# The first output tile stored in one piece, and the early small writes of the output removed, in a masked softmax

## Chip, cores, metric

The kernel runs on one core of one Trainium2 chip. The time is the device time of a run in microseconds (us). A trace is of one profiled run; its span is about 1.8 us shorter than the run's time.

## The reference

Sixteen batches of 8 x 256 rows of 256 numbers; batch b is softmaxed over its first `lengths[b]` columns (128 to 255), and the rest is zero.

```python
for b in range(batch):
    length = lengths[b]
    masked = x[b, :, :, :length].copy()
    masked = masked - np.max(masked, axis=-1, keepdims=True)
    exp_masked = np.exp(masked)
    result[b, :, :, :length] = exp_masked / np.sum(exp_masked, axis=-1, keepdims=True)
```

The input has 33.6 MB and the output too. The kernel reads 28.5 MB of the one, as most tiles are loaded only up to the column needed, and writes all of the other.

## The kernel before

A batch is one tile: 128 partitions, each with `nt` = 16 rows of 256 numbers, 16 KB per partition and 2 MB in all. There are 8 slots. SP loads tiles 0 to 3 and then issues all the stores, everything on one DMA queue (queue 1). GpSimd loads tiles 4 to 15 on another (queue 0). VectorE masks and divides, ScalarE takes the exponential.

How a tile's store is cut decides the packet size: a half of a tile is 8 KB in a row of each partition, a quarter 4 KB, a whole tile 16 KB.

```python
def parts(b):
    if b < 10:
        cuts = [0, half, half + quarter, nt]
    elif b < 12 or b == batch - 1:
        cuts = [0, half, nt]
    else:
        cuts = [0, nt]
    return [slice(i, j) for i, j in zip(cuts, cuts[1:])]
```

The small writes at the top: sixteen times 64 B into the region of tile 0, before anything else is written.

```python
out_e = out_f[0].rearrange("(e r) t k -> e r t k", e=few)[:, 0, 0, :few]
nc.vector.memset(touch, 0.0).then_inc(s_zero, 1)
nc.scalar.wait_ge(s_zero, 1)
nc.scalar.dma_start(out=out_e, in_=touch).then_inc(s_touch, 16)
# [SP's loads of tiles 0 to 3 left out]
nc.sync.wait_ge(s_touch, 16)
for b in range(batch):
    s_b = s_st[b % 2]
    for s in parts(b):
        nc.sync.wait_ge(s_out, 2 * b + (s.stop - 1) // half + 1)      # divided by VectorE
        if b >= 2 and s.start == 0:
            nc.sync.wait_ge(s_b, 64 * (b // 2 + 1))                    # the store of tile b - 2
        nc.sync.dma_start(out=out_f[b, :, s, :], in_=xt[:, b % slots, s, :]
                          ).then_inc(s_b, 16 * ((s.stop - s.start) // quarter))
```

VectorE's order: it masks tile b + 1 (and so waits for that tile's load) before it divides tile b.

```python
for b in range(batch):
    if b == 0:
        divide(0, 0)
    if b + 1 < batch:
        mask(b + 1, slice(0, nt))
    if b > 0:
        divide(b, 0)
    divide(b, 1)
```

The softmax here doesn't subtract the row's maximum and nothing guards it: scores larger than these inputs give would overflow.

## Time and profile before

| | before |
|---|---|
| time, median of 3 runs | 156.84 us (156.65 to 157.08) |
| span of the profiled run | 155.0 us |
| busiest compute engine | VectorE, 74% |
| DMA queues 1 and 0, share of the 16 engines' time | 66.2% and 32.0% |
| mean rate | 400 GB/s |

The two shares of the queues are the row to look at: added, they are 98% of all the time that the 16 DMA engines have. The lines themselves stand in the prediction.

### The profile page before, as it was taken

The page shows a single profiled execution, that of the slowest core. Times are in us where ns is not written, and L with a number is a line of the kernel's source. Part 1 is how long each engine was busy: PE and PEld are TensorE (multiplying, and loading weights), DVE is VectorE, ACT ScalarE, POOL GpSimd, SP SyncE. Part 2 cuts the span into 40 slices and gives each one's busy share as a digit, 9 for nine tenths or more (in the row PEclk, how much of TensorE's full clock was granted, in tenths as well). Part 3 has the DMA queues.
Part 4 walks back from the last instruction along what each step waited for, and adds up shares of the span by engine and source line. Part 5 has one row for each costly group of instructions (what it writes and reads, how often), then busy time and mean ns, then how long its engine had stood idle before and what let it go on. Part 6 is the DMA issues. An engine that isn't in the chain of part 4 may idle for free.

```text
span 155.0 us, 1322 instructions
## 1 busy us (share of the span) xinstructions
PE 0.2 (0%) x1; PEld 0.1 (0%) x1; DVE 115.1 (74%) x85; ACT 105.2 (68%) x514; POOL 19.0 (12%) x25
## 2 busy tenths in 40 slices
PE   0000000000000000000000000000000000000000
PEld 0000000000000000000000000000000000000000
DVE  1249999957999894949889499999894999950000
ACT  3087799993989694793959488989695798800000
POOL 4910031002020201102020112020100000000000
DMA  4999999999999999999999999999999999999993
GB/s 112 421 452 419 444 309 374 417 429 435 403 409 396 411 413 407 429 407 411 410 413 420 404 419 403 408 412 412 425 405 449 420 419 429 440 435 435 416 419 129
DMA packets 10452, 62.08 MB, mean 400 GB/s; under 512 B 930, under 2 KB 1026, under 8 KB 7122
## 3 DMA queue, kind: packets, MB, share of 16 engines
q1 hardware_dynamic: 6336, 41.95, 66.2%
q0 software_dynamic: 4080, 20.12, 32.0%
q14 instruction: 2, 0.02, 0.0%
q10 hardware_dynamic: 34, 0.00, 0.0%
HBM read 28.51 MB, written 33.56 MB: 400 GB/s over the span
## 4 chain that ended last, share of the span: by engine, by line
DMA 66%; DVE 15%; issue 5%; POOLq 2%; SPq 1%; DVEq 0%
DMA xt<-in_x_dram 58%; DVE xt L231 10%; DMA out_dram<-xt 8%; DVE xt L204 5%; DVE inv_sum L228 1%; SPq L117 1%; POOLq L144 0%; POOLq L139 0%; POOLq L101 0%; SPq L119 0%; SPq L127 0%; DVEq L221 0%; POOLq L166 0%; POOLq L162 0%; POOLq L168 0%
## 5 line engine op out<-in xcount | busy, mean ns | idle before, releaser
L258 ACT ACTIVATE xt<-xt x256 | 102.4, 401 | 27.7 <-DVE xt L204 27.7
L231 DVE TENSOR_TENSOR xt<-xt,inv_sum 128x2048 f32<-128x2048 f32 x32 | 73.3, 2292 | 1.1
L204 DVE SCALAR_TENSOR_TENSOR xt<-down,len_s,xt 128x2048 f32<-128x2048 f32 (+1 forms) x17 | 37.8, 2224 | 18.3 <-DMA xt<-in_x_dram 18.2
L258 ACT ACTIVATION_READ_ACCUMULATOR xt<-xt x256 | 47.9, 187 | 0.0
L139 POOL DMA_DIRECT2D xt<-in_x_dram x12 | 12.8, 1064 | 90.0 <-DMA out_dram<-xt 50.4
L228 DVE RECIPROCAL inv_sum<-row_sum 128x8 f32<-128x8 f32 x32 | 6.3, 196 | 1.1 <-ACT xt L258 1.1
L158 POOL MEMSET xt<- 128x1536 f32 x4 | 5.3, 1386 | 1.1 <-DVE len_s L195 1.1
L250 ACT ACT_TABLE_LOAD x1 | 1.3, 1283 | 2.1 <-DVE touch L112 2.1
L112 DVE MEMSET touch<- 16x16 f32 x1 | 0.1, 72 | 1.2 <-SPq L79 1.2
L187 DVE TENSOR_SCALAR down<-iota_i 128x256 f32<-128x256 int32 x1 | 0.3, 297 | 0.3 <-POOL iota_i L150 0.3
L192 DVE CAST len_b<-word 1x16 bf16<-1x16 int32 x1 | 0.2, 163 | 0.4 <-DMA word<-in_lengths_dram 0.4
L195 DVE TENSOR_SCALAR len_s<-len_f 128x16 f32<-128x16 f32 x1 | 0.2, 173 | 0.3 <-PE len_f L174 0.3
L150 POOL IOTA iota_i<- 128x256 int32 x1 | 0.3, 331 | 0.6 <-SPq L79 0.6
L155 POOL MEMSET seed<- 1x1 f32 x2 | 0.3, 162 | 0.0
L250 ACT ACTIVATE warm<-const-float32-0.0 128x1 f32<-128x1 f32 x1 | 0.2, 203 | 0.0
L153 POOL MEMSET ones<- 1x128 bf16 x1 | 0.2, 194 | 0.0
L174 PE MATMUL len_f<-len_b,ones 1*128 1x16 bf16 x1 | 0.2, 166 | 2.6 <-DVE len_b L192 2.6
L276 POOL MEMSET const-float32-0.0<- 128x1 f32 x1 | 0.1, 98 | 0.3 <-issue 0.3
L174 PEld LDWEIGHTS len_f<-len_b,ones 1*128 1x128 bf16 x1 | 0.1, 100 | 2.6 <-POOL ones L153 2.6
L276 POOL MEMSET const-bfloat16-1.0<- 128x1 bf16 x1 | 0.1, 99 | 0.0
L276 POOL MEMSET const-uint8-127<- 128x1 uint8 x1 | 0.1, 99 | 0.0
L276 POOL MEMSET const-float32-1.0<- 128x1 f32 x1 | 0.1, 98 | 0.0
(1 smaller groups left out, 0.0 us busy)
## 6 DMA issues: line engine op xcount, KB each, us to landing
out_dram<-xt SPq DMA_DIRECT2D x16, 1024.0 KB
out_dram<-xt SPq DMA_DIRECT2D x20, 512.0 KB
xt<-in_x_dram SPq DMA_DIRECT2D x3, 2048.0 KB, 16.1
out_dram<-xt SPq DMA_DIRECT2D x3, 2048.0 KB
xt<-in_x_dram POOLq DMA_DIRECT2D x3, 1728.0 KB, 16.2
xt<-in_x_dram POOLq DMA_DIRECT2D x2, 2048.0 KB, 16.2
xt<-in_x_dram POOLq DMA_DIRECT2D x2, 1600.0 KB, 14.2
xt<-in_x_dram POOLq DMA_DIRECT2D x2, 1280.0 KB, 13.6
```

Source lines behind the costliest of these rows:

```text
L117: nc.sync.dma_start(out=xt[:, 0, s], in_=x_f[0, :, s]).then_inc(s_ld[h], 16)
L139: nc.gpsimd.dma_start(out=xt[:, slot, :, :w], in_=x_n[:, n, :, :w]).then_inc(s_sw[par], 16)
L150: nc.gpsimd.iota(iota_i, pattern=[[1, seq_k]], base=0, channel_multiplier=0).then_inc(s_iota, 1)
L155: nc.gpsimd.memset(seed[:, par : par + 1], 0.0).then_inc(s_st[par], 64)
L158: nc.gpsimd.memset(xt[:, b, :, low:], 0.0).then_inc(s_fill, 1)
L174: nc.tensor.matmul(len_f, lhsT=ones, rhs=len_b, start=True, stop=True).then_inc(s_lenf, 1)
L204: return nc.vector.scalar_tensor_tensor(out=t, in0=down[:, None, lo:hi].to_broadcast([P, s.stop - s.start, hi - lo]), scalar=len_s[:, b : ...
L228: step(nc.vector.reciprocal(out=inv_sum[:, b, s], in_=row_sum[:, b, s]))
L231: nc.vector.tensor_tensor(out=t, in0=t, in1=inv_sum[:, b, s, None].to_broadcast([P, half, seq_k]), op=ALU.mult,).then_inc(s_out, 1)
L250: nc.scalar.activation(out=warm, in_=nc.const_aps.tensor(0.0, (P, 1), F32), func=EXP)
L258: ins = nc.scalar.activation(out=e, in_=e, func=EXP, accum_out=sum_h[:, bass.ds(i, 1), j])
L276: nc = _bacc.Bacc("TRN2", target_bir_lowering=False, num_devices=1)
```

## The change

Its intent: fewer and larger packets for the first tile's store, and no writes at the top that serve nothing but to be early. The diff, cut to its core:

```diff
     def parts(b):
-        if b < 10:
+        if b == 0:
+            cuts = [0, nt]
+        elif b < 10:
             cuts = [0, half, half + quarter, nt]
...
-    few = 16
-    touch = pool.tile([few, few], F32, name="touch")
...
-        out_e = out_f[0].rearrange("(e r) t k -> e r t k", e=few)[:, 0, 0, :few]
-        nc.vector.memset(touch, 0.0).then_inc(s_zero, 1)
-        nc.scalar.wait_ge(s_zero, 1)
-        nc.scalar.dma_start(out=out_e, in_=touch).then_inc(s_touch, 16)
...
-        nc.sync.wait_ge(s_touch, 16)
         for b in range(batch):
```

More of the change, by code (lines that the diff above doesn't have):

```diff
@@ L82 @@
         s_ones = sem("s_ones")
-        s_touch = sem("s_touch")
-        s_zero = sem("s_zero")
         s_lenb = sem("s_lenb")
```

## The prediction

> **What bounds the kernel now.** I read the page's two share lines first, then the windows by stage, then the waits of the store queue, and last the transfers around the first store.
>
> The busy shares, then the slices of the DMA engines:
>
> ```profile
> PE 0.2 (0%) x1; PEld 0.1 (0%) x1; DVE 115.1 (74%) x85; ACT 105.2 (68%) x514; POOL 19.0 (12%) x25
> ...
> DMA  4999999999999999999999999999999999999993
> GB/s 112 421 452 419 444 309 374 417 429 435 403 409 396 411 413 407 429 407 411 410 413 420 404 419 403 408 412 412 425 405 449 420 419 429 440 435 435 416 419 129
> ...
> q1 hardware_dynamic: 6336, 41.95, 66.2%
> q0 software_dynamic: 4080, 20.12, 32.0%
> ```
>
> No compute engine is over 74% busy, while the 16 DMA engines are at nine tenths or more in every slice but the first and the last. Queue 1 carries the first four loads and all stores, queue 0 the GpSimd loads; together they hold 98% of the engines' time. So the end is set by the sum of DMA work, unless a queue runs dry. The windows (stretch, length, busy time of five engines, clock, DMA share, GB/s) show one hole only:
>
> ```profile
> 2.00:20.00 18.00, 0.17 (x1) 0.10 (x1) 11.26 (x10) 11.43 (x51) 5.33 (x4) 1.00 1.01 412
> 20.00:24.00 4.00, 0.00 (x0) 0.00 (x0) 3.93 (x5) 4.00 (x21) 1.29 (x1) 1.00 0.92 281
> 24.00:152.00 128.00, 0.00 (x0) 0.00 (x0) 99.53 (x70) 89.77 (x444) 11.48 (x11) 1.00 1.02 417
> 125.50:152.00 26.50, 0.00 (x0) 0.00 (x0) 12.30 (x10) 8.78 (x44) 0.00 (x0) 1.00 1.01 429
> ```
>
> From 20 to 24 us the engines move 281 GB/s instead of about 415 (share 0.92: they are mostly occupied, but each packet takes longer). That loses (415 - 281) x 4 / 415 = 1.3 us. The first-tile store lies exactly behind it in queue 1. The last row is 26.5 us of stores alone: at the end a deep backlog drains.
>
> Waits of the store queue, over the whole span and then from 120 us on, and the last work of VectorE:
>
> ```profile
> SPq L126 <- DMA out_dram<-xt: 100.5, 14, 11.6
> SPq L127 <- DVE xt L231: 11.6, 6, 4.2
> SPq L124 <- DVE xt L231: 10.2, 1, 10.2
> ...
> SPq L126 <- DMA out_dram<-xt: 28.7, 5, 11.4
> SPq L131 <- DMA out_dram<-xt: 8.1, 1, 8.1
> ...
> 135.64 2.29 DVE L231 TENSOR_TENSOR xt<-xt,inv_sum 128x2048 f32<-128x2048 f32 x1
> 138.92 6.42 SPq L127 DMA_DIRECT2D out_dram<-xt  x3
> ```
>
> SP mostly waits for the store two tiles earlier (L126), hardly for compute. VectorE ends at 135.64 + 2.29 = 137.9 us, and by the last row the final stores are issued up to 138.92 + 6.42 = 145.3 us: the last tile had been ready some 6 us before it was let go. L124, the first wait of SP for compute, took 10.2 us and hurt nobody, as the loads were still running. No row waits at L121 for the small writes: that wait was over before SP came to it.
>
> **What the Trainium skill says.** "HBM Reference", Access, puts one core streaming alone at about 425 GB/s, bounded by its 16 DMA engines; the 429 above agrees. "DMA: Bandwidth & Descriptors", Why small descriptors are slow, gives every packet a small fixed overhead. The trace agrees, and it is tiny at these sizes (sizes below). The same page, Queues, rings and completion order, says that each engine goes round-robin over its queues, switching at packet boundaries; with both queues loaded the trace has packets one for one:
>
> ```profile
> q0 software_dynamic: 193, 0.93, 56.9%
> q1 hardware_dynamic: 195, 0.73, 44.9%
> ```
>
> (DMA queues, 27 to 31 us: queue, packets, MB, share.) So a queue's share of the bytes goes with its packet size. The page speaks of packets of several descriptors; the rows here are single contiguous runs (4096 B of a store, 4800 B of a load).
>
> **The change, part by part.**
>
> Packets: a row of the tile is 16 KB per partition, 8 partitions per DMA engine. The time of a packet, from windows with one size in them: 138 to 142 us has 104 packets of 16 KB at 99.4% of 16 x 4 us, so 0.612 us each; 127.8 to 130 us has 114 of 8 KB at 100.6% of 16 x 2.2 us, so 0.310; 41 to 41.4 us has 42 of 4 KB at 105.8% of 16 x 0.4 us, so 0.161. The first tile's store costs an engine now 8 x 0.310 + 16 x 0.161 = 5.06 us, afterwards 8 x 0.612 = 4.90. Saved: 0.16 us, on the bound.
>
> Small writes: 16 writes of 64 B and their 16 completions, on queue 10. The DMA queues between 5.3 and 6.7 us, and their issue:
>
> ```profile
> q10 hardware_dynamic: 32, 0.00, 1.4%
> ...
> out_dram<-touch ACTq DMA_DIRECT2D x1, 1.0 KB, 5.3
> ```
>
> 1.4% of 1.4 us is 0.02 us of each engine. The 5.3 us to landing were spent queueing behind the loads, beside which nothing waits. Saved: 0.02 us. The removed VectorE memset (72 ns), and ACT's issue before its table load, lie in a time when both only wait for the first tile. Saved: nothing.
>
> Issues: two SP issues fewer, 0.4 us each, off the path. The one store now waits for both halves (divided by 18.7 us) instead of starting at 14.1. But queue 1 holds four loads ahead of it until about 23.4 us (8 MB from 2.2 us, with the slow stretch), so it starts when it did.
>
> Moved: from about 26.3 us the first GpSimd load shares the engines. Now it meets 64 KB of 4 KB packets, 16 turns an engine until 31.8 us. Afterwards the store is down to about four packets of 16 KB then; the load gets 4 turns in 4 x (0.612 + 0.185) = 3.2 us, then tile 1's 8 KB packets. Its 21 packets an engine (1600 KB / 16 / 4800) then end about 2.5 us later than the 35.6 us of now, and the store of tile 0 about 2.3 us earlier. The bytes are the same, so this is a swap of order.
>
> Sum of what is certain: -0.16 - 0.02 = -0.18 us, or 156.66.
>
> **Rivals.**
>
> First, a cold output. The small writes look put there to make the first access to the output early. Without them the real stores may begin with slow packets. For it: the first reads of the input were slow. Between 2 and 4 us the four half-microseconds moved 246, 147, 262 and 328 GB/s, a mean of 246, which against 429 loses 0.85 us (ramp included). Against it: the small writes themselves show no stall around them (416 GB/s in 5.3 to 6.7 us), and only 16 spots were touched. If it holds, an estimate of its cost is the same 0.85 us, so 157.5; 40%.
>
> Second, a wait that takes the freed one's place. The first GpSimd load lands 2.5 us later, VectorE waits for it longer than its 2.6 us of now, and everything behind shifts: up to +2.3 us, 159. Against it: the DMA engines have stores of tiles 1 to 3 to move meanwhile, and the final tile has some 6 us to spare. 10%.
>
> Third, the slow stretch from 20 to 24 us hangs on the stores waiting behind the loads, and goes or shrinks with their new form: up to -1.3, so 155.5. For it: it ends where the stores begin. Against it: the first GpSimd issue falls in the same stretch (20.85 us) and stays. 12%.
>
> **Range and chances.** -0.18 + 0.4 x 0.85 + 0.1 x 2.3 - 0.12 x 1.3 = +0.23, which I round down: 157.0 us. The range is from the third rival, a little short of full, to the first with twice its estimated size: 155.9 to 158.5. Two per cent are 3.1 us: slower needs two rivals together, or a cold start of over 3 us, 4%; faster would need more than the whole hole at 20 us, 1%.
>
> **What would show it.** Right: queue 10 falls from 34 packets to 2, queue 1 loses 16 data packets, DMA stays at nine tenths in all middle slices, the last tile still waits for its predecessor's store. The swap: the first GpSimd load's time to landing grows from 14.7 to about 17 us, with the end unmoved. The cold output: GB/s between 23 and 28 us well under 400, packets of 16 KB over 0.612 us there. The prediction is wrong if the DMA share sinks anywhere behind 28 us, if the last store is issued straight from VectorE, or if the stretch from 20 to 24 us changes by over 1 us.

## The result

The changed kernel took 156.40 us (median of 4 runs, 156.32 to 156.85), the kernel before 156.80 beside it (4 runs). The ratio is 0.9978, with a 95% interval of 0.9954 to 1.0002. A ratio here is the mean time of one kernel's fast runs over the mean of the other's in the same rounds, so it is not quite the ratio of the medians. Executions over 1.5% slower than the fastest of the same kernel are left out of the means. By the 2% rule the two are the same; whether the small gain is real is a question for the experiments.

The page of the changed kernel, first engine shares, then the DMA slices, then the queues (queue, packets, MB, share):

```profile
PE 0.2 (0%) x1; PEld 0.1 (0%) x1; DVE 115.1 (74%) x84; ACT 105.2 (68%) x514; POOL 19.0 (12%) x25
...
DMA  4999999999999999999999999999999999999993
GB/s 108 430 445 424 436 309 416 409 411 436 423 404 388 423 405 416 412 412 422 398 421 412 411 413 404 414 409 412 417 409 450 417 420 426 443 432 436 424 415 144
...
q1 hardware_dynamic: 6048, 41.95, 66.1%
q0 software_dynamic: 4080, 20.12, 32.1%
...
q10 hardware_dynamic: 2, 0.00, 0.0%
```

Nothing has moved at this distance. VectorE has one instruction less (the memset). Queue 10 fell from 34 packets to 2, as the small writes were 16 data packets and 16 completions. Queue 1 has 6336 - 6048 = 288 packets less: 256 of data (16 engines times 24 before, times 8 now) and two completions per engine, 32. The prediction's list says "16 data packets", which is right per engine.

The same windows of the changed kernel (stretch, length, busy time of five engines, clock, DMA share, GB/s), and the waits of its store queue:

```profile
2.00:20.00 18.00, 0.16 (x1) 0.10 (x1) 11.25 (x10) 11.10 (x51) 5.33 (x4) 1.00 1.00 411
20.00:24.00 4.00, 0.00 (x0) 0.00 (x0) 3.93 (x5) 4.00 (x21) 1.71 (x2) 1.00 0.97 303
24.00:152.00 128.00, 0.00 (x0) 0.00 (x0) 99.62 (x70) 89.75 (x444) 11.09 (x11) 1.00 1.01 417
```

```profile
SPq L117 <- DMA out_dram<-xt: 98.9, 14, 9.6
SPq L118 <- DVE xt L222: 24.7, 7, 14.9
SPq L122 <- DMA out_dram<-xt: 8.2, 1, 8.2
```

The slow stretch at 20 to 24 us is still there, at 303 GB/s after 281, and all behind it runs at 417 as before. The first wait of SP for compute is now under L118, 14.9 us long in place of 10.2: the store waits for both halves of the tile, behind loads that still run, at no cost.

What did move is the first GpSimd load. The first row is VectorE's mask of tile 4 before the change, the second the same after it (in brackets: idle time of VectorE before it, and what ended it):

```profile
35.83 2.35 DVE L204 SCALAR_TENSOR_TENSOR xt<-down,len_s,xt 128x2048 f32<-128x2048 f32 x1 [2.62 <-DMA xt<-in_x_dram]
```

```profile
37.59 2.35 DVE L195 SCALAR_TENSOR_TENSOR xt<-down,len_s,xt 128x2048 f32<-128x2048 f32 x1 [4.40 <-DMA xt<-in_x_dram]
```

The load lands 1.8 us later, and VectorE waits 1.8 us longer. The reason shows in the queues from 26.2 to 29.2 us of the changed kernel:

```profile
q1 hardware_dynamic: 62, 0.92, 71.5%
q0 software_dynamic: 64, 0.31, 24.7%
```

The packets stand one for one, but queue 1's are 16 KB and queue 0's 4.8 KB, so the load gets a quarter of the engines' time instead of about half. And the end is where it was:

```profile
137.17 2.29 DVE L222 TENSOR_TENSOR xt<-xt,inv_sum 128x2048 f32<-128x2048 f32 x1
...
138.59 6.31 SPq L118 DMA_DIRECT2D out_dram<-xt  x3
```

VectorE ends at 139.5 us instead of 137.9, while the last stores still go out up to 144.9 us (145.3 before).

### The profile page after: what moved, and what is told of

It reads as the page before. It is cut to its first block, busy times and chain, and to the rows that moved or that the text cites. A ratio compares the mean times of both kernels' runs of the same rounds, so it can differ in the third digit from the quotient of the medians.

```text
span 154.7 us, 1317 instructions
## 1 busy us (share of the span) xinstructions
PE 0.2 (0%) x1; PEld 0.1 (0%) x1; DVE 115.1 (74%) x84; ACT 105.2 (68%) x514; POOL 19.0 (12%) x25
## 3 DMA queue, kind: packets, MB, share of 16 engines
q1 hardware_dynamic: 6048, 41.95, 66.1%
## 4 chain that ended last, share of the span: by engine, by line
DMA 71%; DVE 12%; issue 4%; POOLq 1%; SPq 1%; DVEq 0%
DMA xt<-in_x_dram 60%; DMA out_dram<-xt 11%; DVE xt L222 9%; DVE xt L195 3%; SPq L109 1%; POOLq L135 1%; DVE inv_sum L219 0%; POOLq L130 0%; SPq L111 0%; SPq L118 0%; POOLq L157 0%; POOLq L159 0%; DVEq L212 0%; POOLq L137 0%; SPq L278 0%
```

## The experiments

Twelve kernels ran in four batches, each batch on one chip beside runs of the kernel before. Times are medians; "before" is its median in the same batch.

| run | time (us) | before (us) | ratio to before, 95% interval | GB/s, 20 to 24 us |
|---|---|---|---|---|
| after_again | 156.53 | 156.84 | 0.9984 (0.9967 to 1.0001) | 324 |
| no_touch_only | 156.84 | 156.84 | 1.0006 (0.9987 to 1.0025) | 295 |
| whole_only | 156.88 | 156.84 | 1.0013 (0.9990 to 1.0036) | 336 |
| whole_first4 (5 fast runs) | 159.09 | 156.84 | 1.0157 (1.0119 to 1.0194) | 320 |
| gpsimd_later | 157.32 | 156.96 | 1.0029 (1.0006 to 1.0052) | 303 |
| stores_later | 158.06 | 156.96 | 1.0072 (1.0049 to 1.0095) | 292 |
| gpsimd_tiny_first | 156.85 | 156.96 | 0.9999 (0.9981 to 1.0018) | 315 |
| sp_touch | 156.92 | 156.79 | 0.9996 (0.9975 to 1.0017) | 332 |
| sp_touch_rows | 157.00 | 156.79 | 1.0004 (0.9981 to 1.0026) | 299 |
| tail_quarters | 157.30 | 156.79 | 1.0027 (1.0002 to 1.0051) | 332 |
| after_third | 156.55 | 156.97 | 0.9981 (0.9957 to 1.0006) | 315 |
| whole_first2 | 157.53 | 156.97 | 1.0029 (1.0003 to 1.0056) | 332 |

### The change again, and its two parts

after_again and after_third are the changed kernel as it is.

> The changed kernel once more, as the yardstick of this job. Theory (packets): the whole gain is the first tile's eight 16 KB packets in place of 8 KB and 4 KB ones, plus 0.02 us of small writes: 0.2 us under the kernel before, ratio 0.9987. The first reading (0.9978, or 0.35 us) would be partly chance. Rival (slow stretch): the change also shortens the stretch from 20 to 24 us (303 GB/s after 281), so 0.35 us again, with over 300 GB/s in it.

> The changed kernel a third time, since neither part alone showed its share and 0.2 us is near what five rounds can tell. Theory (packets): ratio 0.9988; with the first two readings (0.9978, 0.9984) the mean of the three stays below 1 but within 0.3 us of it. If it reads 1.000 or more, the first two were mostly chance of the run.

The three readings are 0.9978, 0.9984 and 0.9981, a mean of 0.9981, or 0.3 us of 156.8. Each interval taken alone just reaches past 1 (upper ends 1.0002, 1.0001 and 1.0006), but three batches agree. So the small gain is most likely real. It is so small, though, that kernels which differ from the changed one by a few small instructions (whole_only, gpsimd_tiny_first, sp_touch, sp_touch_rows, all below) read 0.9996 to 1.0013. Nor does it name its cause: after_again gained 0.25 us with 324 GB/s in the slow stretch, which lies between the two theories of its expectation (0.2 us, or 0.35 us with over 300 GB/s).

no_touch_only removes the small writes alone:

```diff
-        if b == 0:
-            cuts = [0, nt]
-        elif b < 10:
+        if b < 10:
```

(against the changed kernel).

> Only the small writes at the top are gone; the first tile is stored in three parts as before. Theory: 0.02 us of DMA work less, which no timing shows: ratio 1.000 within 0.001, and the windows from 23 to 28 us as in the kernel before. Rival (cold output): the first real stores are slow, packets of 8 KB above 0.31 us from 23 us on beyond the 0.33 to 0.42 us that the kernel before shows in its first microsecond, up to 0.85 us lost: ratio 1.005.

It took 156.84 us, as the kernel before did, and its windows from 24 to 28 us move 412 GB/s against 411. No cold start of the output appears where the small writes are gone. A slowing of 0.85 us would be a ratio of 1.005; the interval ends at 1.0025.

whole_only makes the first store whole and keeps the small writes:

```diff
-        if b < 10:
+        if b == 0:
+            cuts = [0, nt]
+        elif b < 10:
             cuts = [0, half, half + quarter, nt]
```

(against the kernel before).

> Only the first tile's store is made whole; the small writes stay. Theory (packets): 0.16 us less than before, ratio 0.999, so nearly the whole of the change's gain; the first GpSimd load lands at about 37.4 us as in the changed kernel. Rival: the small writes cost more than their 0.02 us, then this is slower than the changed kernel by over 0.15 us.

The load landed as late as in the changed kernel (VectorE's mask of tile 4 starts at 37.62 us). The time, though, reads 156.88 and not below before: three of its six runs lie at 156.6 and three at 157.2 to 157.4. Its interval, 0.9990 to 1.0036, holds 0.999 only at its edge. Its median is 0.35 us above after_again in the same batch, so the rival's condition, small writes that cost more than 0.15 us, is met by the numbers; but taking them away alone gained nothing. The two parts do not add up to the whole by these readings. A spread of 0.9 us within one kernel's runs leaves a difference of 0.2 us unresolved, and I do not read a cause into it.

### The packet cost by itself

To see the packet cost without a change of order, tail_quarters cuts tiles 12 to 14, which are stored when no load runs any more:

```diff
         else:
-            cuts = [0, nt]
+            cuts = [0, quarter, half, half + quarter, nt]
```

> The changed kernel with tiles 12 to 14 stored in four parts each (4 KB packets) instead of whole (16 KB). Nothing loads beside them, so this is the packet cost by itself, with no change of order against a load. By the packet times, an engine pays 3 x (32 x 0.161 - 8 x 0.612) = 0.77 us more: ratio to the changed kernel 1.005, or about 157.2 us. If packet sizes do not count, it stays at 156.4 to 156.5, and the packet part of the prediction falls.

The ratio to before is 1.0027; against the 0.9981 of the changed kernel that is 0.0046 x 156.8 = 0.72 us, where 0.77 was expected (through two intervals of some 0.25%, so it is a rough match). The changed kernel itself did not run in this batch; against its two near copies that did, sp_touch and sp_touch_rows, the difference is only 0.3 to 0.4 us. The trace is finer. From 138 to 142 us, packets and queue 1, first with 16 KB packets (the changed kernel), then with 4 KB (this run):

```profile
DMA packets 110, 1.72 MB, mean 430 GB/s; under 512 B 5, under 2 KB 5, under 8 KB 5
...
q1 hardware_dynamic: 110, 1.72, 100.4%
```

```profile
DMA packets 461, 1.68 MB, mean 419 GB/s; under 512 B 52, under 2 KB 52, under 8 KB 461
...
q1 hardware_dynamic: 461, 1.68, 102.3%
```

105 packets of 16 KB took 100.4% of 16 x 4 us, 0.612 us each; 409 packets of 4 KB took 102.3%, 0.160 us each. Four small ones cost 0.640, so a 16 KB row costs about 5% more in 4 KB pieces. The packet term of the prediction stands.

### More of the same: two and four tiles whole

If only the sum of DMA work counted, more whole tiles would be better. whole_first2 and whole_first4 have `b < 2` and `b < 4` in place of `b == 0`.

> The changed kernel with tiles 0 and 1 stored whole, between the one tile that is free and the four that cost 2.8 us. Sum of work alone: 0.16 us below the changed kernel. Order: the first GpSimd load has 12 turns against 16 KB packets (0.80 us each) and the rest against tile 2's 8 KB (0.49 us), an estimate from the packet times that lands it near 40 us, against 37.4 with one tile whole and 43.3 with four. With GpSimd held back the load landed near 41.5 us and the time rose by some 0.8 us over the changed kernel, queue 1 running dry near 48 us; here I expect the same in small: 0 to 0.8 us above the changed kernel, and GB/s between 44 and 52 us under 400 if queue 1 runs dry.

> The changed kernel with tiles 0 to 3 stored whole, four times the packet saving. Theory (only the sum of DMA work counts): four times 0.16 us, so 0.48 us below the changed kernel, ratio 0.996 to before. Rival (order counts): against 16 KB packets the first GpSimd load gets one 4.8 KB turn per 0.80 us and lands near 43 us instead of 37.4; VectorE, and behind it the third and fourth stores, come late, queue 1 runs dry for a while, the DMA share sinks below nine tenths between 45 and 55 us, and the time is above the changed kernel, by up to 2 us.

Both are slower than the changed kernel of their own batch: by 157.53 - 156.55 = 0.98 us and 159.09 - 156.53 = 2.6 us (the 2.8 in an expectation counts the slow run in). The first GpSimd load lands later and later; VectorE's mask of tile 4, with two tiles whole, then with four:

```profile
41.42 2.35 DVE L195 SCALAR_TENSOR_TENSOR xt<-down,len_s,xt 128x2048 f32<-128x2048 f32 x1 [8.21 <-DMA xt<-in_x_dram]
```

```profile
43.57 2.35 DVE L195 SCALAR_TENSOR_TENSOR xt<-down,len_s,xt 128x2048 f32<-128x2048 f32 x1 [10.42 <-DMA xt<-in_x_dram]
```

VectorE's idle time before it goes 2.6 (before), 4.4 (one), 8.2 (two), 10.4 us (four). As VectorE masks tile 4 before it divides tile 3, the store of tile 3 comes late as well, and queue 1 runs dry. The queues from 49 to 51 us with four tiles whole hold one row alone, and the windows show that stretch with two tiles whole and a second hole, at the end, with four:

```profile
q0 software_dynamic: 123, 0.58, 102.2%
```

```profile
48.00:52.00 4.00, 0.00 (x0) 0.00 (x0) 3.97 (x4) 3.35 (x19) 1.15 (x1) 1.00 1.02 336
```

```profile
144.00:146.00 2.00, 0.00 (x0) 0.00 (x0) 1.97 (x3) 2.00 (x12) 0.00 (x0) 1.00 0.27 115
```

The first row is the lesson for reading a DMA share: 102% busy, and yet only 289 GB/s. With nothing but 4.7 KB load packets of GpSimd, each takes 1.022 x 16 x 2 / 123 = 0.27 us; mixed with stores, the 4.8 KB packets of the first load took about 0.19 us (24.7% of 16 x 3 us over 64 packets, in the queue rows of the changed kernel above). So a dry store queue shows less as idle engines than as slow packets. Only the last hole, in which nothing is left to load, is idle (share 0.27).

So the DMA sum holds as long as queue 1 has stores in hand, and one whole tile lies inside that, two do not. My landing estimate for two tiles was near 40 us; it landed at about 41.2, just before VectorE's mask at 41.42.

### Where the slow stretch at 20 to 24 us comes from

It costs about 1.3 us in the kernel before and could hide or fake a result of this size. Three runs ask for its owner: the first GpSimd load (issue at 20.8 us), or the stores queued behind the loads. All start from the changed kernel.

gpsimd_later:

```diff
-        nc.gpsimd.wait_ge(s_ld[ahead - 1], 16)
+        nc.gpsimd.wait_ge(s_ld[ahead], 16)
```

> The changed kernel, with GpSimd waiting for the fourth tile of the input instead of the third before its first load (issue near 26 us instead of 20.8). It asks where the slow stretch from 20 to 24 us comes from. If from the first GpSimd load: the stretch is at 420 GB/s now, and a stretch of about 260 to 300 GB/s comes at 26 to 29 us. If from the stores queued behind the loads: it stays where it was. If from the addresses or the time of the fourth tile's reads: it stays too. Time: not better than 156.4, as the first GpSimd load comes 5 us later, though the DMA engines have stores to move.

stores_later:

```diff
+        nc.sync.wait_ge(s_ld[ahead], 16)
         for b in range(batch):
             s_b = s_st[b % 2]
```

> The changed kernel, with the store queue waiting for the fourth tile of the input to land before it issues the first store. If the slow stretch from 20 to 24 us comes from stores queued behind the loads, it goes to 420 GB/s; if from the first GpSimd load at 20.8 us, it stays near 300. A hole of some 2 us at about 24 us follows in either case, as queue 1 is empty between the loads' landing and the first store: 1.5 to 2.5 us slower.

The windows from 20 to 22 us of the changed kernel, of gpsimd_later and of stores_later, in this order:

```profile
20.00:22.00 2.00, 0.00 (x0) 0.00 (x0) 1.97 (x3) 2.00 (x11) 1.16 (x1) 1.00 1.16 328
```

```profile
20.00:22.00 2.00, 0.00 (x0) 0.00 (x0) 1.97 (x3) 2.00 (x12) 0.00 (x0) 1.00 1.19 319
```

```profile
20.00:22.00 2.00, 0.00 (x0) 0.00 (x0) 1.97 (x3) 2.00 (x11) 1.19 (x1) 1.00 1.01 434
```

With GpSimd out of the way (its first issue is at 26.96 us) the stretch stays: 319. With the stores held back (first store issued at 23.54 us) the loads of the fourth tile run on at 434. So the last loads are slow when a store stands behind them on the queue, and GpSimd's issue is not needed for it (one trace each). I had used GpSimd's issue as the argument against this rival; that argument falls. The whole window from 20 to 24 us is no test in stores_later (292 GB/s), as it holds the hole that follows the loads.

Nor is it shown that the slowing vanished there. The first store was issued at 23.54 us, but no packet of a store had started by 27 us, and the GpSimd load ahead of it ran slowly (282 GB/s from 25 to 28 us). From 26 to 27 us:

```profile
q0 software_dynamic: 47, 0.23, 111.4%
```

That is 1.114 x 16 / 47 = 0.38 us for each packet, where the same 4.8 KB took about 0.19 beside stores, and packets of about this size some 0.27 alone. So the slowing may have moved with the first store rather than gone; loads that run alone explain only part of it.

gpsimd_later also took 157.32 us, ratio 1.0029: it is a second way of making the first GpSimd load late (VectorE idle for 8.5 us), and its window from 47 to 51 us falls to 333 GB/s, as with two tiles whole.

gpsimd_tiny_first has a tiny early GpSimd DMA:

```diff
+        nc.gpsimd.dma_start(out=tiny, in_=lengths[None, :]).then_inc(s_tiny, 16)
         nc.gpsimd.wait_ge(s_v, 2)
...
         nc.gpsimd.wait_ge(s_word, 16)
+        nc.gpsimd.wait_ge(s_tiny, 16)
```

> The changed kernel with a tiny GpSimd DMA (128 B of lengths into a tile of its own) near 2 us. If the slow stretch is a first-use cost of GpSimd's DMA, it is paid in the ramp at the start: 20 to 24 us at 400 GB/s or more, and up to 1.1 us faster than the changed kernel (155.3). If it is the cost of writing one load's descriptors, it stays at about 300 GB/s, and the time is unchanged within 0.2 us. If the stores cause it: unchanged too.

Nothing moved: 315 GB/s and 156.85 us, which fits the stores as the cause.

Two more runs try to pay that cost early, with small writes on queue 1 itself: sp_touch with the sixteen writes of 64 B, sp_touch_rows with 256 B to each of the 128 rows. The edit, shortened:

```diff
         for h in range(2):
             s = slice(h * half, (h + 1) * half)
             nc.sync.dma_start(out=xt[:, 0, s], in_=x_f[0, :, s]).then_inc(s_ld[h], 16)
+        nc.vector.memset(touch, 0.0).then_inc(s_zero, 1)
+        nc.sync.wait_ge(s_zero, 1)
+        nc.sync.dma_start(out=<16 x 64 B, or 128 x 256 B, of tile 0>, in_=touch).then_inc(s_touch, 16)
         for b in range(1, ahead):
             nc.sync.dma_start(out=xt[:, b], in_=x_f[b]).then_inc(s_ld[b + 1], 16)
+        nc.sync.wait_ge(s_touch, 16)
```

The writes stand after both halves of tile 0's load and ahead of tile 1's, not between the halves as the first expectation says; for the question it is the same.

> The changed kernel with the sixteen 64 B writes back, but issued by SP on queue 1, between the two halves of the first tile's load, so ahead of the other loads. The runs with the store queue or GpSimd held back say that the slow stretch goes before the first real store, wherever that stands. If it is the first write of queue 1 (whatever its size), it moves to the top, 20 to 24 us runs at over 400 GB/s, and the time falls by up to 1 us where the top hides it, or stays where not. If it belongs to the first large store, or to memory not written before, 20 to 24 us stays near 310 GB/s and the time within 0.3 us of the changed kernel.

> As the run before, with 256 B written to each of the 128 partitions' rows (and so eight writes an engine, both halves' addresses). If the slow stretch is the first access to each row's output memory, 20 to 24 us rises to over 380 GB/s here but not with sixteen writes. If it is the large store as such, neither moves it, and the time is that of the changed kernel plus 0.05 us.

The stretch stays at 332 and 299 GB/s, as in the other runs with a whole first tile, and the times (156.92 and 157.00) are not below the changed kernel's. Neither a write of queue 1 nor a write to each row pays the cost early. What it is about the first real stores that slows the loads ahead of them remains open. Also open is whether the form of the store matters to it: the two kernels with the split store show 281 and 295 GB/s, the eleven with a whole one 299 to 336, 319 in the mean (stores_later left aside). The difference of the means, 31 GB/s, would be 31 x 4 / 415 = 0.3 us. But two traces against eleven, which scatter by 37 GB/s among themselves, do not settle it, though the edges of the window are not the reason: from 16 to 28 us the same two show 375 and 376 GB/s, the eleven 379 to 398. So a part of the measured gain may come from here and not from the packet sizes.

No experiment gave a version that beats the changed kernel.

## Why the prediction was right

**The sum.** -0.18 us was worked out, and about -0.3 us was measured (mean ratio of three batches 0.9981). The packet term holds in the trace of tail_quarters to a hundredth of a microsecond per packet; in its time the three tiles cost 0.3 to 0.7 us, by the yardstick taken, where 0.77 was worked out. The term of the small writes, 0.02 us, agrees with no_touch_only, which is not faster than before. The clock does not resolve the two terms from each other, nor from a slow stretch that may have become a little shorter, which the sum left out. That the time came out near the sum does not prove the sum.

**The swap of order.** The load was to land 2.5 us later, with a time to landing of about 17 us. It landed 1.8 us later, and its landing took 16.5 us (14.7 before). The turns were the right ones, but the number set on them was not worked out to its end: 4 turns to 29.5 us, then 8 of 0.310 + 0.185 to 33.5, then the other 9 against 4 KB, 0.345 each, lead to about 36.6 us. The same working for the kernel before, 16 turns against 4 KB and 5 against 8 KB, gives 26.3 + 16 x 0.345 + 5 x 0.495 = 34.3, not the 35.6 that was measured. So, like for like, it gives a shift of 2.3 us; 2.5 was a little much, and 1.8 was measured. The end of the kernel did not move with it, as said.

**First rival, the cold output (40%, 0.85 us).** It fell. Stores run at 420 GB/s from 24 to 28 us in the changed kernel (411 before), and no_touch_only shows no loss. The other sign that was named, packets of 16 KB over 0.612 us, does show, but it does not depend on the small writes: from 24 to 26 us they took 0.62 us each in the changed kernel (102.5% of 16 x 2 us over 53) and 0.63 in whole_only, which keeps the small writes (105.5% over 54). I gave it too much weight: the small writes' mere presence counted as an argument. Without it the centre would have been 156.7, nearer to the 156.4 measured.

**Second rival, VectorE late (10%).** It did not happen with one tile, and happens with two and four, by the predicted path. But the margin that I named was the wrong one. The "6 us to spare" of the last tile is a margin at the end. With two tiles whole, the load came another 3.8 us later than in the changed kernel, less than those 6 us, and it cost a microsecond all the same, because queue 1 ran dry at 48 to 52 us. The other half of the argument, that stores of tiles 1 to 3 fill the time, is the true margin, and it is shorter.

**Third rival, the slow stretch (12%).** Its link to the stores was right, as stores_later shows, but its new form brought at most a few tenths, not 1.3 us.

**Two readings to put right, without effect on the sum.** The prediction calls the 4800 B of a load a single contiguous run. The load has 1600 KB in 128 x 16 rows, so a row has 800 B, and a packet of 4800 B is six rows. And the 425 GB/s of "HBM Reference" stands under Specifications (TRN2), not Access.

So the range held, since no rival took effect; the centre of 157.0 was 0.6 us too high, through weights on rivals and not through the sum.

## What to carry to other kernels

Where the DMA engines are busy throughout, count packets by size and by duration: that sum was right to a few tenths here, and early writes or late issues behind a full queue were worth nothing. Larger packets on one queue take turns away from the other, so ask how long the queues behind the delayed load stay fed, in mid-run and not only at the end. A gain of 0.2% needs several batches before it may be called one.

## What the Trainium skill lacked or had wrong

- "DMA: Bandwidth & Descriptors", Queues, rings and completion order, speaks of round-robin by packets of several descriptors. The loads agree (a packet of 4800 B is six rows of 800 B), while a store's packet here is one run of 4 to 16 KB. The two queues moved about one packet for one whatever the sizes (193 against 195 with 4.8 and 4 KB; 64 against 62 with 4.8 and 16 KB, completions counted), so the share of a queue follows the size of its packets. The page does not say this of the share.
- No page has what GpSimd loads of short rows cost without stores beside them: 4.7 KB packets of such rows took 0.27 us alone (289 GB/s at a busy share of 102%), and 4.8 KB packets about 0.19 us mixed with stores. SP's loads of 16 KB packets ran at 411 GB/s alone. "DMA: Bandwidth & Descriptors", Measured, has 425 GB/s for large GpSimd loads, without the length of the runs.
- No page has the slowing of loads ahead of the first stores on the same queue: 311 to 360 GB/s from 20 to 22 us in the thirteen traces with stores queued behind them, 434 in the one with the stores held back.
- "DMA: Bandwidth & Descriptors", Specifications, gives a GpSimd DMA about 1 us to the first byte. Here the first load was issued at 20.84 us, and no packet of its queue had appeared by 26 us. In stores_later, issued at 20.81, the first came at 22.8 us, 2.0 us after the issue. So the delay is not the writing of descriptors alone; it was longer where the other queue had stores waiting.
